# Scan of a Mamba-2 block: the sample's decay factors of all heads made once, in diagonal blocks, and the first set's factors issued one projection later

## The chip, the cores and the metric

The kernel runs on one core of a Trainium2 chip. Five engines with their own instruction queues work side by side: TensorE (PE, with its weight loads shown as PEld), VectorE (DVE), ScalarE (ACT), GpSimd (POOL) and SyncE (SP, which here only issues DMAs). Each takes its instructions in the order in which the program was built. The metric is the device time of one execution in microseconds; the time of a kernel is the median of its runs.

## The reference

One layer of a hybrid trunk for 256 prompt rows and 32 rows of one running stream ("the sample"), 288 rows in all, handled together in fp32.

```python
xn   = rmsnorm(x, norm_mix_pre)
proj = xn @ w_in  # -> [u_pool (1024) | z (2048) | xBC (2560) | dt (32)]
pool = multi-scale trailing-mean mixer on u_pool
ssd  = Mamba-2 mixer: causal conv on xBC, SiLU, exact chunked scan, SiLU gate by z, grouped rmsnorm
x    = x + rmsnorm(concat[pool, ssd] @ w_out, norm_mix_post)
x    = x + rmsnorm(ConvFFN(rmsnorm(x, norm_ffn_pre)), norm_ffn_post)
```

The change is in the scan. For each of 32 heads (64 channels each; two groups of 16 heads share B and C) and for a chunk with running sums `acum` of dt*A:

```python
lmat   = exp(where(causal, acum[l] - acum[s], -inf))
y_diag = einsum(C.B[l, s] * lmat[l, s], x[s] * dt[s])      # within the chunk
y_off  = einsum(C, h_prev, exp(acum))                      # from the state before
```

The sample is a chunk of 32 rows whose state before is an input (`state_ssd`); the prompt starts from zero.

## The kernel before, in words

**Matmuls.** Every fp32 product is made of three: weights and activations are split into a high and a low part, and `mm3` (L145, L146, L147) adds high by high, high by low and low by high. Weights come in DMAs of 1 MB; `split_w` turns each into two pieces of 128x1024, the high part `whi` on ACT (L138) and the low part `wlo` on DVE (L139). There are four buffers for each part. A projection of 256 columns (`project`, K16) takes two DMAs, hence four pieces of 24 matmuls: 96 matmuls on PE.

**Order of the mixer.** First the B/C and first x columns; then seven projections of x (i = 1 to 7), then eight of z (scan steps 8 to 15). After each projection stand, in program order, the evictions of its two accumulators (`ebuf`, L360 and L361 on DVE, for x; `z`, L556, for z), the causal convolution of the tiles of the projection before (`xs_conv`), and `scan(i)`. The convolved x goes to DRAM (`xs_d`) by DMAs on POOL's queue. The framework then orders each engine's instructions by a simulated timeline; weight pieces and evictions have a raised priority.

**The scan.** Heads are taken in eight sets of four. `SCAN_IN` names the steps after which a set's factors are made (`four_in`), `SCAN_OUT` those after which the ready sets, two at a time, are multiplied (`four_out`). `four_in` loads with SP the running sums broadcast to all partitions (`gb`), the state `h0t` and the set's x with rows on partitions (`xw`: two blocks of 128 prompt rows, and a third block of the last 128 rows, of which the last 32 are the sample's). Then, per set:

- ACT: `ce` = Exp of the sample's sums (L487); twelve Relus (L497), per head one of 256, one of 128 and one of 32 columns, `m` = relu(sum of row s - sum of column l); one Exp of the whole `m`, 4 x 416 = 1664 columns (L500). DVE: `ce` times C (L490), `xw` times dt (L493, 768 columns), `m` times the masked B.C products `cbt` (L502, 1664 columns).

`gb`, `xw`, `ce` and `m` have two buffers each, so the third set writes where the first was. `four_out` issues per set sixteen matmuls into `py` (L524), four heads for each of k = 0 to 3: k = 0, 256 prompt columns with `xw` block 0 and `m`; k = 1, 128 columns with block 1; k = 2, the sample's 32 columns with block 2 and `m`; k = 3, the sample's 32 columns with the state and `ce`. They keep their program order on PE, behind the projection. The first run of `four_out` is at step 7: sets 0 and 1, made at steps 5 and 6.

Of the kernel before, what the change touches and what calls it, by code (L numbers as in the profile page):

```python
# [8 lines left out]
F32 = mybir.dt.float32  # L9
F32R = mybir.dt.float32r  # L10
AF = mybir.ActivationFunctionType
ALU = mybir.AluOpType
# [4 lines left out]
P = 128  # L17
TC = {"schedule_with_timeline_sim": True}
D_MODEL = 2048
NP_ = 256  # L20
NS = 32
NT = NP_ + NS
# [3 lines left out]
HEADS = 32  # L26
# [10 lines left out]
MW = 416  # L37
# [6 lines left out]
def body(  # L44
# [25 lines left out]
    act, dve, pool, pe, sp = nc.scalar, nc.vector, nc.gpsimd, nc.tensor, nc.sync  # L70
# [45 lines left out]
        return t[:, 58 : 58 + n * nc_].rearrange("p (k c) -> p k c", k=n)  # L116

    ahead = [0]

    def fetch_w(view, kb, nk, c0, nc_):  # L120
        raw = wpool.tile([P, nk, nc_], F32, tag="raw", name="raw")
# [4 lines left out]
    def split_w(raw, kb, nk, nc_, after=()):  # L126

        out = []
        step = min(nk, 1024 // nc_)
        for k in range(0, nk, step):  # L130
            n = min(step, nk - k)
            hi = wtile("hi", n, nc_)
            lo = wtile("lo", n, nc_)
            with ExitStack() as order:
                order.enter_context(tc.high_priority(offset=ahead[0]))
                for ins in after:
                    order.enter_context(tc.issue_after(ins.ins))
                act.activation(hi, raw[:, k : k + n, :], AF.Copy)  # L138
                dve.tensor_tensor(lo, raw[:, k : k + n, :], hi.bitcast(F32), op=ALU.subtract)  # L139
            out.append([(kb + k + i, hi[:, i, :], lo[:, i, :]) for i in range(n)])  # L140
        return out

# [35 lines left out]
    def blocks_out(d, t, src, pool_, bufs=1, eng=None):  # L178
# [47 lines left out]
    start = ExitStack()  # L226
# [38 lines left out]
    for kb, n in chunks:  # L265
        raw = wpool.tile([P, n, 768], F32, tag="raw", name="raw")
# [19 lines left out]
        for k in range(kb, kb + n):  # L286
# [11 lines left out]
            hi, lo = wtile("hi", 1, 768)[:, 0, :], wtile("lo", 1, 768)[:, 0, :]  # L298
            step = 256 if k < 2 else 768
            for c in range(256 if k == 0 else 0, 768, step):  # L300
                w_hi = act.activation(hi[:, c : c + step], raw[:, k - kb, c : c + step], AF.Copy)
# [9 lines left out]
            for m in range(2 if k == 0 else 0, 6):  # L311
                c = slice(m * P, (m + 1) * P)
# [37 lines left out]
    last_in = [None]  # L350
# [81 lines left out]
    tok = mp.tile([P, 3, 2, HEADS], F32, name="tok")  # L432
    tokd = const.tile([P, 3, HEADS], F32, name="tokd")
    dec_s = mp.tile([HEADS, 4, NS], F32, name="dec_s")
    dve.tensor_copy(dec_s, dec[:, NP_:].unsqueeze(1).broadcast_to([HEADS, 4, NS]))
    dec_s = dec_s.rearrange("h r s -> h (r s)")
    def tok_out():
        p_ = aux([P, 3, 3, HEADS], "ptok")
        jobs = [(2, 2, dec_s)] + [(b, 2, dec[:, P * b : P * b + P]) for b in range(2)]
        for b, (go, o) in enumerate(((0, 0), (256, P), (288, NT - P))):  # L440
# [5 lines left out]
        dve.tensor_copy(tok, p_[:, :, 0:2, :])  # L446
        dve.tensor_copy(tokd, p_[:, :, 2, :])

    tok_out()

# [3 lines left out]
        conv_out(NX + i, bc_in[i], o)  # L454
        bc.append(o)
    b_d = dram.tile([NT, 2 * P], F32, name="b_d")
    cbt = mp.tile([P, 2, MW], F32, name="cbt")
    pool.memset(cbt, 0.0)
    for gi in range(2):
        blocks_out(b_d, gi, bc[gi], mp, 3)  # L460
        p_ = aux([P, MW], "pcb")
        pe.matmul(p_[:, 0:256], bc[gi][:, 0:P], bc[2 + gi][:, 0:NP_], start=True, stop=True)
        pe.matmul(p_[:, 256:384], bc[gi][:, P:NP_], bc[2 + gi][:, P:NP_], start=True, stop=True)
        pe.matmul(p_[:, 384:], bc[gi][:, NT - P :], bc[2 + gi][:, NP_:], start=True, stop=True)
# [3 lines left out]
        dve.tensor_tensor(cbt[P - NS :, gi, 384:], p_[P - NS :, 384:], tri[P - NS :, P - NS :], op=ALU.mult)  # L468


    xs = []
# [2 lines left out]
    def four_in(q):  # L474

        c = slice(2 * P * q, 2 * P * q + 2 * P)
        gb = mp.tile([P, 4, MW], F32, tag="gb", bufs=2, name="gb")
        sp.dma_start(out=gb, in_=g_d[4 * q : 4 * q + 4, :].unsqueeze(0).broadcast_to([P, 4, MW]))
        h0t = mp.tile([P, 2 * P], F32, tag="h0t", bufs=2, name="h0t")
        sp.dma_start(out=h0t, in_=state_ssd[:, c])  # L480
        xw = mp.tile([P, 3, 2 * P], F32, tag="xw", bufs=2, name="xw")
        sp.dma_start(out=xw[:, 0:2, :], in_=xs_d[:NP_, c].rearrange("(b p) c -> p b c", p=P))
        sp.dma_start(out=xw[:, 2, :], in_=xs_d[NT - P :, c])
        ce = mp.tile([P, 4, NS], F32, tag="ce", bufs=2, name="ce")
        m = mp.tile([P, 4, MW], F32, tag="m", bufs=2, name="m")
        with tc.issue_after(last_in[0].ins):
            act.activation(ce, gb[:, :, 384:], AF.Exp)  # L487
            act.activation(elast[:, 4 * q : 4 * q + 4], gb[:, :, MW - 1], AF.Exp)
            cs = bc[2 + q // 4][:, NP_:]
            dve.tensor_tensor(ce, ce, cs.unsqueeze(1).broadcast_to([P, 4, NS]), op=ALU.mult)  # L490
            w = tok[:, :, 1, 4 * q : 4 * q + 4].unsqueeze(3).broadcast_to([P, 3, 4, 64])
            x4 = xw.rearrange("p b (r q) -> p b r q", r=4)
            dve.tensor_tensor(x4, x4, w, op=ALU.mult)  # L493
            for j in range(4):
                h = 4 * q + j
                for b, (lo_, hi_) in enumerate(((0, 256), (256, 384), (384, MW))):
                    act.activation(  # L497
                        m[:, j, lo_:hi_], gb[:, j, lo_:hi_], AF.Relu, bias=tok[:, b, 0, h : h + 1], scale=-1.0
                    )
            act.activation(m, m, AF.Exp, scale=-1.0)  # L500
            gi = q // 4
            got = dve.tensor_tensor(m, m, cbt[:, gi : gi + 1, :].broadcast_to([P, 4, MW]), op=ALU.mult)  # L502
        return xw, h0t, ce, m, got

    def four_out(q, ys, xw, h0t, ce, m, _, after=None):

        ops = []
        for k in range(4):
            for j in range(4):
                c = slice(64 * j, 64 * j + 64)  # L510
                y = ys[j // 2][64 * (j % 2) : 64 * (j % 2) + 64, :]
                if k == 0:
                    ops.append((y[:, 0:256], xw[:, 0, c], m[:, j, 0:256], True, False))
                elif k == 1:
                    ops.append((y[:, 128:256], xw[:, 1, c], m[:, j, 256:384], False, True))
                elif k == 2:
                    ops.append((y[:, 256:], xw[:, 2, c], m[:, j, 384:], True, False))
                else:
                    ops.append((y[:, 256:], h0t[:, c], ce[:, j, :], False, True))
        for y, w_, v_, go, end in ops:  # L520
            with ExitStack() as order:
                if after is not None:
                    order.enter_context(tc.issue_after(after.ins))
                ins = pe.matmul(y, w_, v_, start=go, stop=end)  # L524
# [56 lines left out]
    fours = list(range(NX // 2))  # L581
    gates = list(range(NX))
    done = [-1]
    ready = []
# [757 lines left out]
```

## Time and profile before

| what | value |
|---|---|
| median of 3 runs | 1232.44 us (1232.38 to 1233.84) |
| the profiled execution | 1231.95 us, span 1230.2 us |
| PE busy | 1223.2 us, 99% of the span |
| DVE, ACT, POOL busy | 72%, 55%, 23% |
| projection 7 of x | ends on PE at 130.12 us of the span, where `py` starts; 96 matmuls about 0.122 us apart |
| the four runs of `py` on PE | start at 130.12, 157.85, 196.98, 225.51 us, some 3.7 us each |

The span is the time between the first and the last instruction of the profiled execution; the rest of its time lies around it. A row of a group reads: line, engine, operation, output<-inputs, shape of output<-input, count | busy us, mean ns of one | idle time of the engine just before them and what ended it. A row of a timeline reads: start, duration, engine, line, operation, count of neighbours taken together, and in brackets the idle time before it with its releaser. Engines pipeline their instructions, so the next often starts some 0.1 us before the one ahead has ended; the spacing of starts, not the duration, is what an instruction takes of its engine.

### The profile page before, as it was taken

How to read it: one execution, taken by the hardware profiler on the slowest of the kernel's cores; microseconds unless marked ns; L12 is line 12 of the kernel's file. 1: busy time of each engine (PE TensorE's matmuls, PEld its weight loads, DVE VectorE, ACT ScalarE, POOL GpSimd, SP SyncE). 2: the span in 40 equal slices, each digit the busy share in tenths (PEclk: the TensorE clock that was granted, in tenths of full speed). 3: DMA queues.
4: the chain of work that ended last, by engine and by line, in shares of the span. 5: the costliest groups of instructions: out<-in, count | busy, mean ns of one | idle time of the engine just before them, and what ended most of it. 6: DMA issues, size and time to landing. Idle time of an engine off the chain costs nothing.

```text
span 1230.2 us, 25184 instructions
## 1 busy us (share of the span) xinstructions
PE 1223.2 (99%) x10037; PEld 1212.8 (99%) x10037; DVE 888.5 (72%) x1488; ACT 672.2 (55%) x1013; POOL 277.8 (23%) x428
## 2 busy tenths in 40 slices
PE   9999999999999999999999999999999999999998
PEld 9999999999999999999999999999999999999998
DVE  8999998989654599977776744446777776765555
ACT  8558787546544566654554544334455555454443
POOL 6395442141331200321211200001122121201110
PEclk9999999999999999999999999999999999999999
DMA  9668785466666655776555555555555555576763
GB/s 345 217 202 315 255 281 172 150 244 220 204 234 222 194 174 200 222 211 193 198 183 172 165 186 177 170 193 182 195 172 172 182 184 184 172 248 203 226 189 120
DMA packets 87637, 249.95 MB, mean 203 GB/s; under 512 B 45728, under 2 KB 51936, under 8 KB 65248
## 3 DMA queue, kind: packets, MB, share of 16 engines
q1 hardware_dynamic: 83184, 240.78, 58.5%
q0 software_dynamic: 3760, 7.08, 2.0%
q8 instruction: 78, 1.28, 0.4%
q10 hardware_dynamic: 576, 0.49, 0.1%
q14 instruction: 39, 0.32, 0.1%
HBM read 236.36 MB, written 11.95 MB: 202 GB/s over the span
## 4 chain that ended last, share of the span: by engine, by line
PE 91%; DVE 3%; ACT 3%; issue 1%; DMA 1%; ACTq 0%; DVEq 0%
PE acc L147 29%; PE acc L145 29%; PE acc L146 29%; ACT m L497 2%; DVE wlo L139 1%; PE acc_x L146 1%; PE acc_x L145 1%; PE acc_x L147 1%; ACT whi L138 0%; PE py L524 0%; DMA g_d<-g 0%; DMA gb<-g_d 0%; DVE conv L373 0%; PE low L1183 0%; PE run_a L1185 0%
## 5 line engine op out<-in xcount | busy, mean ns | idle before, releaser
L139 DVE TENSOR_TENSOR wlo<-raw,whi 128x1024 fp32r<-128x1024 f32 (+1 forms) x386 | 460.8, 1196 | 242.3 <-ACT whi L138 241.9
L138 ACT ACTIVATE whi<-raw 128x1024 fp32r<-128x1024 f32 (+1 forms) x386 | 397.2, 1032 | 358.4 <-PE acc L146 290.0
L146 PE MATMUL acc<-hn,whi 128*128 128x288 f32 x1360 | 382.5, 286 | 0.0
L147 PE MATMUL acc<-hn,wlo 128*128 128x288 f32 x1360 | 382.5, 286 | 0.0
L145 PE MATMUL acc<-hn,whi 128*128 128x288 f32 x1360 | 381.8, 286 | 0.1
L146 PEld LDWEIGHTS acc<-hn,whi 128*128 128x128 f32 x1360 | 254.6, 189 | 0.1
L147 PEld LDWEIGHTS acc<-hn,wlo 128*128 128x128 f32 x1360 | 254.6, 189 | 0.0
L145 PEld LDWEIGHTS acc<-hn,whi 128*128 128x128 f32 x1360 | 254.0, 189 | 0.6 <-ACT hn L964 0.5
L145 PE MATMUL acc<-xn,whi 128*128 128x288 f32 x686 | 196.6, 288 | 0.0
L146 PE MATMUL acc<-xn,whi 128*128 128x288 f32 x686 | 195.0, 286 | 0.0
L147 PE MATMUL acc<-xn,wlo 128*128 128x288 f32 x686 | 192.2, 287 | 0.9 <-DVE wlo L139 0.4
L145 PE MATMUL acc<-fa,whi 128*128 128x288 f32 x660 | 188.8, 286 | 0.0
L146 PE MATMUL acc<-fa,whi 128*128 128x288 f32 x660 | 188.8, 286 | 0.0
L147 PE MATMUL acc<-fa,wlo 128*128 128x288 f32 x660 | 188.8, 286 | 0.0
L1014 POOL COPY fc_stage<-ebuf 128x4 f32<-128x4 f32 x88 | 30.2, 343 | 467.4 <-DVE ebuf L1013 467.4
L145 PEld LDWEIGHTS acc<-xn,whi 128*128 128x128 f32 x686 | 129.6, 189 | 1.5 <-issue 0.9
L146 PEld LDWEIGHTS acc<-xn,whi 128*128 128x128 f32 x686 | 129.7, 189 | 0.2
L147 PEld LDWEIGHTS acc<-xn,wlo 128*128 128x128 f32 x686 | 127.9, 189 | 1.7 <-DVE wlo L139 0.9
L145 PEld LDWEIGHTS acc<-fa,whi 128*128 128x128 f32 x660 | 124.7, 189 | 0.0
L146 PEld LDWEIGHTS acc<-fa,whi 128*128 128x128 f32 x660 | 124.7, 189 | 0.0
L147 PEld LDWEIGHTS acc<-fa,wlo 128*128 128x128 f32 x660 | 124.7, 189 | 0.0
L1018 ACT ACTIVATE fc<-ebuf,pf 128x290 f32<-128x290 f32 x88 | 54.6, 623 | 77.3 <-DVE ebuf L1013 77.3
(315 smaller groups left out, 1798.4 us busy)
## 6 DMA issues: line engine op xcount, KB each, us to landing
raw<-in_w_up SPq DMA_DIRECT2D x80, 1024.0 KB, 4.8
raw<-in_w_in SPq DMA_DIRECT2D x38, 1024.0 KB, 5.0
raw<-in_w_down SPq DMA_DIRECT2D x32, 1024.0 KB, 4.8
raw<-in_w_out SPq DMA_DIRECT2D x23, 1024.0 KB, 5.0
raw<-in_w_down SPq DMA_DIRECT2D x16, 768.0 KB, 4.4
raw<-in_w_up SPq DMA_DIRECT2D x8, 896.0 KB, 4.6
gb<-g_d SPq DMA_DIRECT2D x8, 832.0 KB, 6.5
raw<-in_w_first SPq DMA_DIRECT2D x5, 768.0 KB, 7.6
```

The source lines that it names most:

```text
L138: act.activation(hi, raw[:, k : k + n, :], AF.Copy)
L139: dve.tensor_tensor(lo, raw[:, k : k + n, :], hi.bitcast(F32), op=ALU.subtract)
L145: pe.matmul(out, wh, hi, start=start, stop=False)
L146: pe.matmul(out, wh, lo, start=False, stop=False)
L147: pe.matmul(out, wl, hi, start=False, stop=stop)
L497: act.activation(m[:, j, lo_:hi_], gb[:, j, lo_:hi_], AF.Relu, bias=tok[:, b, 0, h : h + 1], scale=-1.0)
L1014: pool.tensor_copy(fc_stage[:, :, :, i], e[:, 256:324].rearrange("p (s c) -> p s c", c=34)[:, :, 0:2])
L1018: act.activation(c, e[:, 0:290], AF.Identity, bias=pf[:, 3, i : i + 1], scale=pf[:, 0, i : i + 1])
```

## The change: what it does

The sample's part leaves `m`, and is made for all heads at once.

- `m` has 4 x 384 columns. Per set, the four Relus of 32 columns go; the Exp and the product with `cbt` have 1536 columns, the product of `xw` with dt 512. The third `xw` block is not loaded; instead `xw_s`, 128x64, holds the set's sample rows, head j on partitions 32j to 32j+31.
- `ms` (128 x 8 sets x 32 columns) holds the sample's factors of all 32 heads, again head j of a set on partitions 32j to 32j+31. Four DMAs on POOL's queue load the sums, and `sample_factors()`, called once at step 6, makes the rest: a subtraction on DVE (L501), Relu and Exp on ACT (L502, L503), two products with `cbs` (B.C of the sample) and one with dt on DVE. Then four ACT copies (L510, 32 partitions x 256 columns) write them into `msz` (128 x 4 x 8 x 32), which was zeroed before: copy j fills rows 32j to 32j+31 of block j alone.
- The k = 2 matmuls read `xw_s` and block j of `msz`. Since the other rows of the block are zero, the same 128 rows of `xw_s` serve all four heads.
- Around it: `tok` loses its third block; `tok_s` (four small ACT copies), `g_s4`, `dt_s4`, `dec_s` and `b_s4` are copies of the sample's columns repeated four times, made on ACT, so that transposes and the B.C product (`pcb`) give the four-fold layout; `tri_s` is the mask, by four POOL copies.

`four_in` is cut into loads (`four_in`) and arithmetic (`four_mul`). At step 5 only set 0's loads are issued. Its arithmetic stands at the start of `scan(6)`, after the second weight piece of projection 6 (`splits[-3]`) and the last eviction. Sets 1 to 7 have both in one step as before.

```diff
@@ split_w
+            splits.append((w_hi, w_lo))
@@ the sample's factors
+    ms = mp.tile([P, 8, NS], F32, name="ms")
+    msz = mp.tile([P, 4, 8, NS], F32, name="msz")
+    pool.memset(msz, 0.0)
+    for j in range(4):
+        pool.dma_start(
+            out=ms[NS * j : NS * (j + 1)],
+            in_=g_d.rearrange("(q j) c -> j q c", j=4)[j, :, 384:].unsqueeze(0).broadcast_to([NS, 8, NS]),
+        )
+
+    def sample_factors():
+        each = lambda t: t.unsqueeze(2).broadcast_to([P, 8, NS])
+        with tc.issue_after(last_in[0].ins):
+            dve.tensor_tensor(ms, each(tok_s[:, 0, :]), ms, op=ALU.subtract)
+            act.activation(ms, ms, AF.Relu)
+            act.activation(ms, ms, AF.Exp, scale=-1.0)
+            for gi in range(2):
+                q4 = slice(4 * gi, 4 * gi + 4)
+                dve.tensor_tensor(ms[:, q4], ms[:, q4], cbs[:, gi : gi + 1, :].broadcast_to([P, 4, NS]), op=ALU.mult)
+            dve.tensor_tensor(ms, ms, each(tok_s[:, 1, :]), op=ALU.mult)
+            for j in range(4):
+                r_ = slice(NS * j, NS * (j + 1))
+                act.activation(msz[r_, j], ms[r_], AF.Copy)
@@ four_in and four_mul
-        xw = mp.tile([P, 3, 2 * P], F32, tag="xw", bufs=2, name="xw")
-        sp.dma_start(out=xw[:, 0:2, :], in_=xs_d[:NP_, c].rearrange("(b p) c -> p b c", p=P))
-        sp.dma_start(out=xw[:, 2, :], in_=xs_d[NT - P :, c])
+        xw = mp.tile([P, 2, 2 * P], F32, tag="xw", bufs=2, name="xw")
+        sp.dma_start(out=xw, in_=xs_d[:NP_, c].rearrange("(b p) c -> p b c", p=P))
+        xw_s = mp.tile([P, 64], F32, tag="xw_s", bufs=2, name="xw_s")
+        sp.dma_start(out=xw_s, in_=xs_d[NP_:, c].rearrange("s (j c) -> j s c", j=4))
...
-        m = mp.tile([P, 4, MW], F32, tag="m", bufs=2, name="m")
-        with tc.issue_after(last_in[0].ins):
+        m = mp.tile([P, 4, MW], F32, tag="m", bufs=2, name="m").rearrange("p j c -> p (j c)")
+        m = m[:, : 4 * CW].rearrange("p (j c) -> p j c", j=4)
+        return gb, xw, xw_s, h0t, ce, m
+
+    def four_mul(q, gb, xw, xw_s, h0t, ce, m, after):
...
-                for b, (lo_, hi_) in enumerate(((0, 256), (256, 384), (384, MW))):
+                for b, (lo_, hi_) in enumerate(((0, 256), (256, CW))):
@@ four_out
-                    ops.append((y[:, 256:], xw[:, 2, c], m[:, j, 384:], True, False))
+                    ops.append((y[:, 256:], xw_s, msz[:, j, q, :], True, False))
@@ scan
+    def four_next(after):
+        q, tiles = loads.pop(0)
+        ready.append((q, four_mul(q, *tiles, after)))
+
     def scan(i):
+        if loads:
+            four_next((*splits[-3], last_in[0]))
...
-            ready.append((q, four_in(q)))
+            loads.append((q, four_in(q)))
+            if i > 5:
+                four_next((last_in[0],))
+        if i == 6:
+            sample_factors()
```

**The first run of `py` on PE.** Behind projection 7 in the order before (`m_1633` is set 0's factors, py_1995 and py_1996 its outputs):

```order
L524 MATMUL py_1995<-m_1633,xw_1629 64x256 x2
L524 MATMUL py_1996<-m_1633,xw_1629 64x256 x2
L524 MATMUL py_1995<-m_1633,xw_1629 64x128 x2
L524 MATMUL py_1996<-m_1633,xw_1629 64x128 x2
L524 MATMUL py_1995<-m_1633,xw_1629 64x32 x2
L524 MATMUL py_1996<-m_1633,xw_1629 64x32 x2
L524 MATMUL py_1995<-ce_1632,h0t_1627 64x32 x2
L524 MATMUL py_1996<-ce_1632,h0t_1627 64x32 x2
```

and now (`m_1659` is set 0's):

```order
L575 MATMUL py_2024<-m_1659,xw_1654 64x256 x2
L575 MATMUL py_2025<-m_1659,xw_1654 64x256 x2
L575 MATMUL py_2024<-m_1659,xw_1654 64x128 x2
L575 MATMUL py_2025<-m_1659,xw_1654 64x128 x2
L575 MATMUL py_2024<-msz_844,xw_s_1656 64x32 x2
L575 MATMUL py_2025<-msz_844,xw_s_1656 64x32 x2
L575 MATMUL py_2024<-ce_1658,h0t_1652 64x32 x2
L575 MATMUL py_2025<-ce_1658,h0t_1652 64x32 x2
```

The count and the places are the same; the third pair of rows reads `msz` where it read `m`.

**ACT around that run.** The last `whi` piece of the first z projection and the third set's factors, in the order now (`m_2073` is the third set's, in the buffer of `m_1659`; `ce_2072` its `ce`):

```order
L139 ACTIVATE whi_2154<-raw_2148 128x1024
L548 ACTIVATE m_2073<-gb_2064,tok_734 128x256
L548 ACTIVATE m_2073<-gb_2064,tok_734 128x128
L548 ACTIVATE m_2073<-gb_2064,tok_734 128x256
L548 ACTIVATE m_2073<-gb_2064,tok_734 128x128
L548 ACTIVATE m_2073<-gb_2064,tok_734 128x256
L548 ACTIVATE m_2073<-gb_2064,tok_734 128x128
L548 ACTIVATE m_2073<-gb_2064,tok_734 128x256
L548 ACTIVATE m_2073<-gb_2064,tok_734 128x128
L551 ACTIVATE m_2073<-m_2073 128x1536
L510 ACTIVATE msz_844<-ms_843 32x256 x4
L538 ACTIVATE ce_2072<-gb_2064 128x128
```

The copies into `msz` are new here; before, the third set's Relus stood behind the same piece too, and no py matmul read what came after them.

**DVE in projection 7.** Between the second eviction of projection 6 and the low part of the fourth weight piece of projection 7, before:

```order
L360 TENSOR_TENSOR ebuf5_674<-acc_1653,rstd_124 128x256
L361 TENSOR_TENSOR ebuf5_674<-acc_1653,rstd_124 128x32
L490 TENSOR_TENSOR ce_1817<-ce_1817,bc_772 128x128
L493 TENSOR_TENSOR xw_1814<-xw_1814,tok_734 128x768
L502 TENSOR_TENSOR m_1818<-m_1818,cbt_795 128x1664
L139 TENSOR_TENSOR wlo_1904<-raw_1897,whi_1903 128x1024
```

and now:

```order
L362 TENSOR_TENSOR ebuf5_674<-acc_1661,rstd_124 128x256
L363 TENSOR_TENSOR ebuf5_674<-acc_1661,rstd_124 128x32
L541 TENSOR_TENSOR ce_1658<-ce_1658,bc_781 128x128
L544 TENSOR_TENSOR xw_1654<-xw_1654,tok_734 128x512
L553 TENSOR_TENSOR m_1659<-m_1659,cbt_808 128x1536
L541 TENSOR_TENSOR ce_1840<-ce_1840,bc_781 128x128
L544 TENSOR_TENSOR xw_1836<-xw_1836,tok_734 128x512
L553 TENSOR_TENSOR m_1841<-m_1841,cbt_808 128x1536
L501 TENSOR_TENSOR ms_843<-tok_s_742,ms_843 128x256
L140 TENSOR_TENSOR wlo_1933<-raw_1926,whi_1932 128x1024
```

Set 0's three products and the subtraction of `ms` have come in ahead of the weight piece.

More of the change, by code (lines that the diff above doesn't have):

```diff
@@ L430, in body, with four_times @@
     dve.tensor_tensor(dec, dec, dt, op=ALU.mult)
-    tok = mp.tile([P, 3, 2, HEADS], F32, name="tok")
+    tok = mp.tile([P, 2, 2, HEADS], F32, name="tok")
     tokd = const.tile([P, 3, HEADS], F32, name="tokd")
-    dec_s = mp.tile([HEADS, 4, NS], F32, name="dec_s")
-    dve.tensor_copy(dec_s, dec[:, NP_:].unsqueeze(1).broadcast_to([HEADS, 4, NS]))
-    dec_s = dec_s.rearrange("h r s -> h (r s)")
+    def four_times(src, name):
+        o = mp.tile([HEADS, 4, NS], F32, name=name)
+        act.activation(o, src.unsqueeze(1).broadcast_to([HEADS, 4, NS]), AF.Copy)
+        return o.rearrange("h r s -> h (r s)")
+    g_s4, dt_s4 = four_times(g[:, 384:], "g_s4"), four_times(dt[:, NP_:], "dt_s4")
+    dec_s = four_times(dec[:, NP_:], "dec_s")
+    tok_s = mp.tile([P, 2, 8], F32, name="tok_s")
     def tok_out():
         p_ = aux([P, 3, 3, HEADS], "ptok")
-        jobs = [(2, 2, dec_s)] + [(b, 2, dec[:, P * b : P * b + P]) for b in range(2)]
-        for b, (go, o) in enumerate(((0, 0), (256, P), (288, NT - P))):
+        jobs = [(2, 2, dec_s)] + [(b, 2, dec[:, P * b : P * b + P]) for b in range(2)] + [(2, 0, g_s4), (2, 1, dt_s4)]
+        for b, (go, o) in enumerate(((0, 0), (256, P))):
             jobs += [(b, 0, g[:, go : go + P]), (b, 1, dt[:, o : o + P])]
@@ L456, in body @@
     b_d = dram.tile([NT, 2 * P], F32, name="b_d")
-    cbt = mp.tile([P, 2, MW], F32, name="cbt")
-    pool.memset(cbt, 0.0)
+    b_s4 = []
+    for gi in range(2):
+        t = mp.tile([P, 4, NS], F32, name=f"b_s4{gi}")
+        act.activation(t, bc[gi][:, NP_:].unsqueeze(1).broadcast_to([P, 4, NS]), AF.Copy)
+        b_s4.append(t.rearrange("p r s -> p (r s)"))
+    CW = 384
+    cbt = mp.tile([P, 2, CW], F32, name="cbt")
+    cbs = mp.tile([P, 2, NS], F32, name="cbs")
+    tri_s = mp.tile([P, NS], F32, name="tri_s")
+    for j in range(4):
+        r_ = slice(NS * j, NS * (j + 1))
+        pool.tensor_copy(tri_s[r_, :], tri[r_, r_])
     for gi in range(2):
@@ L463, in body @@
         pe.matmul(p_[:, 256:384], bc[gi][:, P:NP_], bc[2 + gi][:, P:NP_], start=True, stop=True)
-        pe.matmul(p_[:, 384:], bc[gi][:, NT - P :], bc[2 + gi][:, NP_:], start=True, stop=True)
+        pe.matmul(p_[:, 384:], b_s4[gi], bc[2 + gi][:, NP_:], start=True, stop=True)
         dve.tensor_tensor(cbt[:, gi, 0:128], p_[:, 0:128], tri, op=ALU.mult)
@@ L501, in four_in, with four_out @@
             gi = q // 4
-            got = dve.tensor_tensor(m, m, cbt[:, gi : gi + 1, :].broadcast_to([P, 4, MW]), op=ALU.mult)
-        return xw, h0t, ce, m, got
-    def four_out(q, ys, xw, h0t, ce, m, _, after=None):
+            got = dve.tensor_tensor(m, m, cbt[:, gi : gi + 1, :].broadcast_to([P, 4, CW]), op=ALU.mult)
+        return xw, xw_s, h0t, ce, m, got
+    def four_out(q, ys, xw, xw_s, h0t, ce, m, _, after=None):
         ops = []
```

21 lines of the change are left out of this document (15 added, 6 removed).

## The prediction

> **What bounds the kernel now.** I read first the page's engine totals and its chain of work that ended last.
>
> ```profile
> span 1230.2 us, 25184 instructions
> PE 1223.2 (99%) x10037; PEld 1212.8 (99%) x10037; DVE 888.5 (72%) x1488; ACT 672.2 (55%) x1013; POOL 277.8 (23%) x428
> PE 91%; DVE 3%; ACT 3%; issue 1%; DMA 1%; ACTq 0%; DVEq 0%
> PE acc L147 29%; PE acc L145 29%; PE acc L146 29%; ACT m L497 2%; DVE wlo L139 1%; PE acc_x L146 1%; PE acc_x L145 1%; PE acc_x L147 1%; ACT whi L138 0%; PE py L524 0%; DMA g_d<-g 0%; DMA gb<-g_d 0%; DVE conv L373 0%; PE low L1183 0%; PE run_a L1185 0%
> ```
>
> PE is busy for 99% of the span; no other engine is above 72%. The chain gives ACT's Relus (L497) 2%, some 20 us, which looks like an invitation. So I asked next what PE itself waits for in the stretch that the change touches: the list of waits, PE, 84 to 260 us (its only row), then the windows of 10 us, and the timeline at the two gaps that the windows show.
>
> ```profile
> PE acc L147 <- DVE wlo L139: 0.4, 1, 0.4
> ...
> 100.00:110.00 10.00, 10.00 (x83) 9.95 (x82) 8.26 (x25) 8.26 (x27) 5.66 (x12) 1.00 1.03 372
> ...
> 210.00:220.00 10.00, 9.59 (x76) 9.27 (x75) 8.87 (x9) 9.95 (x12) 0.00 (x0) 1.00 0.32 105
> ...
> 152.26 0.19 PEld L147 LDWEIGHTS acc<-xn,wlo 128*128 128x128 f32 x1 [0.30 <-DVE wlo L139]
> ...
> 213.92 0.39 PE L147 MATMUL acc<-xn,wlo 128*128 128x288 f32 x1 [0.41 <-DVE wlo L139]
> ```
>
> Columns of a window: width; busy us (instructions) of PE, PEld, DVE, ACT, POOL; granted clock; DMA share; GB/s. While the Relus of the first two sets of four heads run (100 to 110), PE is busy for all 10 us. In the whole scan PE loses two short stalls, 0.3 and 0.4 us, both for the low part of a weight piece. **So there is at most about 0.7 us to win here**, and the question is whether the change puts a wait on PE that was not there.
>
> **The change part by part.** *Work removed off the path.* These are the factor instructions, grouped by shape, 80 to 250 us.
>
> ```profile
> L497 ACT ACTIVATE m<-gb,tok 128x256 f32<-128x256 f32 x32 | 15.8, 494 | 0.3 <-PE py L524 0.3
> L497 ACT ACTIVATE m<-gb,tok 128x128 f32<-128x128 f32 x32 | 12.4, 386 | 0.0
> L497 ACT ACTIVATE m<-gb,tok 128x32 f32<-128x32 f32 x32 | 9.8, 306 | 0.0
> L500 ACT ACTIVATE m<-m 128x1664 f32<-128x1664 f32 x8 | 12.6, 1575 | 0.0
> L502 DVE TENSOR_TENSOR m<-m,cbt 128x1664 f32<-128x1664 f32 x8 | 15.1, 1888 | 6.7 <-ACT m L500 6.7
> L493 DVE TENSOR_TENSOR xw<-xw,tok 128x768 f32<-128x768 f32 x8 | 8.2, 1027 | 1.1 <-DMA xw<-xs_d 1.1
> ```
>
> All 32 Relus of 32 columns go: 9.8 us of ACT. The Exp loses 128 of 1664 columns, by the step from 128 to 256 columns (494 less 386 ns) 0.11 us each, 0.9 over eight. The product with cbt loses 128 x 1.13 ns (1888/1664) = 0.14, xw's 256 x 1.34 ns (1027/768) = 0.34: 3.9 us of DVE over eight. Added on ACT are some 13 narrow copies (`four_times`, `b_s4`, `tok_s`, `msz`, estimate 0.3 to 0.5 each by the first and third row: 4 to 6 us) and one Relu and Exp of 256 columns (1.0); on DVE four operations of 256 columns (about 1.6). ACT and DVE end a few us lighter, PE has as many matmuls as before; the four new loads of `ms` stand on POOL's queue (POOL is busy for 23%) long before `sample_factors`; SP's loads keep their places, one of 32 KB in place of one of 128. Since PE waits for none of this in its row, all of it is worth 0 on the path, and at the best the 0.7 us above.
>
> *The wait that is added.* The order of the built program decides. Four heads' py runs on PE as eight matmuls with `m`, four with the sample's factors, four with `ce`. The four in the middle now read `msz`, each its own block, and the ACT copies that write `msz` (L510) stand, at the first run, behind the eight Relus and the Exp of `m_2073`, the third set. That set takes over the buffer of `m_1659` (tag "m", two buffers), which is what those eight py matmuls read. So ACT cannot begin the Relus until PE has done the eight, and PE cannot go on with the ninth until ACT has done Relus, Exp and the first copy. Before, no py matmul waited in this place, since its own `m` held the sample's columns. That the reuse does bind, the tile view of `m` says (who waited for PE's py, and for how long):
>
> ```profile
>   PE py L524: 0.3, 1
> ...
>   ACT m L497: 0.3, 1
> ```
>
> Now its price. PE at the first run before, and ACT's spacing:
>
> ```profile
> 129.90 0.29 PE L147 MATMUL acc<-xn,wlo 128*128 128x288 f32 x1
> 130.12 1.73 PE L524 MATMUL py<-m,xw 128*64 128x256 f32 x24
> 131.67 0.41 PE L524 MATMUL py<-ce,h0t 128*64 128x32 f32 x8
> 131.90 0.63 PE L524 MATMUL py<-m,xw 128*64 128x256 f32 x4
> ...
> L524 PE MATMUL py<-m,xw 128*64 128x128 f32 x48 | 4.0, 273 | 0.0
> ```
> ```profile
> 102.06 3.71 ACT L497 ACTIVATE m<-gb,tok 128x256 f32<-128x256 f32 x12
> 105.67 0.29 ACT L487 ACTIVATE ce<-gb 128x128 f32<-128x128 f32 x1
> ...
> 110.02 1.57 ACT L500 ACTIVATE m<-m 128x1664 f32<-128x1664 f32 x1
> 111.51 0.39 ACT L497 ACTIVATE m<-gb,tok 128x128 f32<-128x128 f32 x1
> ...
> 4.66 0.72 ACT L301 ACTIVATE whi<-raw 128x256 fp32r<-128x256 f32 x2 [0.41 <-DMA raw<-in_w_first]
> ...
> 131.33 1.04 ACT L138 ACTIVATE whi<-raw 128x1024 fp32r<-128x1024 f32 x1
> 132.27 1.90 ACT L497 ACTIVATE m<-gb,tok 128x256 f32<-128x256 f32 x6
> ```
>
> Let T be the start of py (130.12 before). The four `ce` matmuls take 131.90 less 131.67 = 0.23; the twelve ahead 1.55; so PE is free after the eight at T+1.32, and the last of them, 273 ns long at a spacing near 0.1, is done at T+1.5. Twelve Relus take 105.67 less 102.06 = 3.61; without the four of 32 columns (306 ns less the overlap of 0.1 = 0.21 each) eight take 2.77. The Exp's spacing is 111.51 less 110.02 = 1.49, less 0.11 = 1.38. Two copies of 256 columns take 0.72, 0.41 for one and 0.31 more for each that follows. The first block is there at T + 1.5 + 0.1 (semaphore, estimate) + 2.77 + 1.38 + 0.41 = T+6.16: PE stands for 4.8 us. Then three blocks at 0.31 feed three matmuls of 0.06: 0.75 more. **Price 5.6 us.** Lower bound: the copies of a quarter of the partitions are no faster in rows I have, but if a copy's end releases earlier and the semaphore costs nothing, 4.9. Upper bound: the last `whi` piece ahead of the Relus ends 0.6 us after PE's eight matmuls, as 131.33 to 132.27 did (T+2.15 against T+1.5), and each block comes at 0.4: 6.4. Queued behind PE's ninth matmul are the rest of py and the whole first z projection; behind ACT's copies the next `ce` and the weight pieces, for which PE has three pieces in hand. The later three runs read a finished `msz` and pay nothing.
>
> *The first run's factors moved.* Set 0's `ce`, `xw` and `m` products now stand on DVE with set 1's in project 7, ahead of the low part of its fourth weight piece (`wlo_1933`); before only set 1's stood there.
>
> ```profile
> 119.76 0.42 DVE L360 TENSOR_TENSOR ebuf<-acc,rstd 128x256 f32<-128x256 f32 x1
> ...
> 122.19 0.42 DVE L360 TENSOR_TENSOR ebuf<-acc,rstd 128x256 f32<-128x256 f32 x1
> 122.62 0.28 DVE L490 TENSOR_TENSOR ce<-ce,bc 128x128 f32<-128x128 f32 x1
> 122.82 0.95 DVE L493 TENSOR_TENSOR xw<-xw,tok 128x768 f32<-128x768 f32 x1
> 123.69 1.88 DVE L502 TENSOR_TENSOR m<-m,cbt 128x1664 f32<-128x1664 f32 x1
> 125.49 1.22 DVE L139 TENSOR_TENSOR wlo<-raw,whi 128x1024 fp32r<-128x1024 f32 x1
> ```
>
> From the second eviction: 0.43, then twice 0.20 + 0.62 (0.87 less a third, rounded up) + 1.66 (1.80 less 0.14), then `ms` 0.33 (the eviction's width) and the piece 1.22: 6.94 us. The second eviction stood 2.43 behind the first; with one of two conv steps (0.4) now ahead of both, 1.95; the first starts between 118.4 (PE's last matmul of project 6, 96 x 0.122 before 130.12) and 119.76. So the piece is ready between 127.3 and 128.7. PE wants it at 130.12 less 24 x 0.122 plus two matmuls, 127.4. **Stall 0 to 1.3, I take 0.5.** Before, the piece was ready at 125.49 + 1.22 = 126.7, 0.7 us ahead, and DVE is busy for all of 120 to 130 (window below): there is no cover for more.
>
> ```profile
> 120.00:130.00 10.00, 10.00 (x84) 9.97 (x82) 10.00 (x17) 4.71 (x7) 6.06 (x6) 1.00 0.60 201
> ```
>
> *The later stalls.* 152.26 and 213.92 keep their cause; DVE is lighter there (0.5 us per set), but z0's pieces follow a stalled ACT. Net 0.1, between -0.7 and +0.5.
>
> **Sum:** 5.6 + 0.5 + 0.1 = +6.2 on the profiled execution of 1231.95 (span 1230.2): 1238.15. The median, 1232.44, is 0.49 above that execution: **1238.6 us**. Bounds: 4.9 + 0 - 0.7 = +4.2 and 6.4 + 1.3 + 0.5 = +8.2, so 1236.6 to 1240.6.
>
> **The rivals.** *The array also slows down after the stall.* 4.8 us without a matmul is longer than any gap of this profile, and how the array restarts shows only at the start:
>
> ```profile
> 0.85 2.90 PE L261 MATMUL idle<-const-float32-1.0 128*128 128x128 f32 x12 [0.85 <-PEq L1316]
> 4.12 2.00 PE L292 MATMUL acc<-xs,raw 128*128 128x288 f32 x4 [0.37 <-DVE xs L290]
> 5.74 0.50 PE L145 MATMUL acc<-xn,whi 128*128 128x288 f32 x1
> ...
> 0.00:10.00 10.00, 8.78 (x48) 7.92 (x49) 4.54 (x11) 6.18 (x14) 3.09 (x32) 1.00 0.78 268
> ```
>
> Until 5.74 a matmul of 288 columns takes 0.50 instead of 0.29, at half pace, though the granted clock reads 1.00 for this window too. From 0.85 on that is 4.9 us at half pace, 2.4 us lost. If the same follows the stall: 1238.6 + 2.4 = 1241.0. For it: the stall is long. Against: a gap of 0.4 us before 4.12 says nothing on when the pace drops. Chance 0.25. [...] The first rows agree with a slow start; no run shown here has a gap that tests the fall.
>
> *The copies are not late* (the change does not wait as I read it): if the third set's Relus did not have to wait for py, they would still follow a `whi` piece of 1.04 that PE's last matmuls (129.90) set free, so the first block would come at 131.1 + 2.77 + 1.38 + 0.41 = T+5.5; the wait vanishes only if the copies overtake the Relus, from T-3 on. Against: ACT takes its instructions in the built order. A part-stall of 0 to 3 us gives 1232.4 to 1235.4. Chance 0.08.
>
> *Faster.* The chain's 20 us of Relus are a real path: its 96 lose 9.8 of 38 us busy, a quarter of 20 = 5 us, so 1227.4. It decides if PE is found waiting where ACT ran the Relus; the window 100 to 110 with PE at 10.00 speaks against. Chance 0.04.
>
> **How the numbers follow.** Forecast 0.60, half pace 0.25, copies not late 0.08, faster 0.04, and 0.03 for more than all that (both stalls at their bounds and half pace, above 1242.6). 0.2%, 2.5 us, is about what a measurement can tell from no change. Slower takes the forecast, half pace, the excess, and a little of the part-stalls: 0.89; same 0.07; faster 0.04. The range reaches from 1235.2, under the lower bound by a missed hiding of about a microsecond, to 1242.6, half pace on the upper part of the second stall.
>
> **What would show it.** Right: one gap of about 5 us on PE within the first py, released by ACT `msz` L510, with the Relus of the third set (L548) on ACT in it, and three short waits behind; below it a wait of some tenths for `wlo` near 127; the other three py phases as before. Records of 0.50 after the gap would make it the half-pace case. Wrong: PE in that py without a gap over 1 us, or a gap before its first matmul (factors not ready) instead of after its eighth.

## The result

The changed kernel takes **1239.96 us** (median of 4 runs, 1238.57 to 1241.03) against 1232.41 for the kernel before (1230.74 to 1233.84): ratio 1.0066, 95% interval 1.0054 to 1.0079. It is slower by 7.55 us. Its profiled execution took 1241.03 us, with a span of 1239.3. Two executions among the experiments below, one of the second and one of the third, took some 1830 us at a clock of 0.654 and are left out of every number here.

The page of the changed kernel (span; busy time of each engine; chain by engine):

```profile
span 1239.3 us, 25192 instructions
PE 1227.2 (99%) x10037; PEld 1217.0 (98%) x10037; DVE 886.4 (72%) x1491; ACT 668.9 (54%) x996; POOL 287.4 (23%) x436
PE 94%; DVE 2%; DMA 1%; ACT 1%; issue 1%; POOL 0%; DVEq 0%; ACTq 0%
```

ACT and DVE did become lighter, by 3.3 and 2.1 us, and the span grew by 9.1. PE's list of waits names the places:

```profile
PE py L575 <- issue: 4.8, 1, 4.8
...
PE acc L149 <- DVE wlo L140: 0.7, 1, 0.7
```

PE's timeline at the first run of `py` (start, duration, instruction, idle time before it). The releaser of the long wait is not named here ("issue"); ACT's rows below give it.

```profile
129.52 0.39 PE L149 MATMUL acc<-xn,wlo 128*128 128x288 f32 x1 [0.74 <-DVE wlo L140]
...
132.17 1.52 PE L575 MATMUL py<-m,xw 128*64 128x256 f32 x16
138.53 1.59 PE L575 MATMUL py<-msz,xw_s 128*64 128x32 f32 x7 [4.84 <-issue]
...
143.49 0.39 PE L147 MATMUL acc<-xn,whi 128*128 128x288 f32 x1
```

ACT's timeline over the same stretch:

```profile
132.15 1.06 ACT L139 ACTIVATE whi<-raw 128x1024 fp32r<-128x1024 f32 x1 [0.94 <-PE acc L148]
133.74 2.88 ACT L548 ACTIVATE m<-gb,tok 128x256 f32<-128x256 f32 x8 [0.53 <-PE py L575]
136.64 1.48 ACT L551 ACTIVATE m<-m 128x1536 f32<-128x1536 f32 x1
138.03 1.72 ACT L510 ACTIVATE msz<-ms 32x256 f32<-32x256 f32 x4
```

The first eight matmuls (each leaves two records, hence 16) start at 132.17; the ninth starts at 138.53, when the first copy into `msz` has ended (138.03 + 0.41). In between ACT waits for PE (0.53), makes the third set's eight Relus and its Exp, and copies. From the start of `py` to the first matmul of the z projection it is 11.32 us, against 3.65 before (130.12 to 133.77).

A part of that is not waiting. The windows of 1 us show the granted clock in the third column from the right:

```profile
136.00:137.00 1.00, 0.00 (x0) 0.00 (x0) 1.00 (x5) 0.97 (x3) 1.00 (x3) 0.51 0.88 349
...
141.00:142.00 1.00, 1.00 (x8) 1.00 (x6) 1.00 (x3) 0.31 (x1) 0.84 (x3) 0.50 1.06 440
142.00:143.00 1.00, 1.00 (x16) 1.00 (x13) 1.00 (x4) 0.57 (x2) 0.32 (x2) 0.58 1.12 336
143.00:144.00 1.00, 1.00 (x23) 0.96 (x18) 1.00 (x6) 0.84 (x3) 0.00 (x0) 1.00 0.90 342
```

The clock is 0.50 from 136.0 to about 142.8, for 6.8 us, of which PE works from 138.5 on. All four runs list a mean clock of 0.997; the 26 runs of the kernel before that stand beside the first four experiments list 0.999 or 1.0.

**Where the 9.1 us of span went**, by the starts of the same work in the two traces:

| stretch | before | after | difference |
|---|---|---|---|
| start to `prs` (first projections) | 37.1 | 38.1 | +1.0 |
| `prs` to the first `py` | 93.0 | 94.0 | +1.0 |
| first `py` to the z projection | 3.65 | 11.32 | +7.67 |
| to the second `py` | 24.1 | 23.7 | -0.35 |
| second to third `py` | 39.1 | 39.1 | 0 |
| third to fourth `py` | 28.5 | 27.85 | -0.7 |
| fourth `py` to the end | 1004.7 | 1005.1 | +0.4 |

`prs` and `psum_g` are short matmuls at the head and in the later part of the mixer, taken as marks. I do not count the first row as the change's: the first matmuls run at half pace (one every 0.24 us here until 9.5 us, then every 0.12), and the end of that stretch lies at 5.7 us in the profile of before, at 9.7 here and between 4 and 7 in the profiles of the first four experiments (8 to 11 matmuls in each us from 5 or 6 us on, 5 or fewer in the us before), so it moves from one profile to another. `prs` starts at 37.1 in the profile of before, at 38.1 here, and at 35.9 to 37.7 in the experiments' profiles; the two do not go together in all of them (36.0 in the third experiment, whose matmuls reach full pace between 5 and 6 us, against 37.1 before with 5.7), so a part of this row is open. The last row, +0.4, stays unexplained. The executions of the kernel before spread by 3.5 us for these reasons or others, which bounds what the comparisons below can tell.

### The profile page after: what moved, and what is told of

The parts are those of the page before. It is cut to its first block, busy times and chain, and to the rows that moved or that the text cites. A ratio compares the mean times of both kernels' runs of the same rounds, so it can differ in the third digit from the quotient of the medians.

```text
span 1239.3 us, 25192 instructions
## 1 busy us (share of the span) xinstructions
PE 1227.2 (99%) x10037; PEld 1217.0 (98%) x10037; DVE 886.4 (72%) x1491; ACT 668.9 (54%) x996; POOL 287.4 (23%) x436
## 4 chain that ended last, share of the span: by engine, by line
PE 94%; DVE 2%; DMA 1%; ACT 1%; issue 1%; POOL 0%; DVEq 0%; ACTq 0%
PE acc L147 30%; PE acc L149 30%; PE acc L148 30%; PE py L575 1%; PE acc_x L149 1%; PE acc_x L147 1%; PE acc_x L148 1%; DMA sx<-xs_d 1%; ACT m L548 0%; DVE wlo L140 0%; PE py_a L575 0%; PE low L1244 0%; PE run_a L1246 0%; POOL xs_d L186 0%; ACT whi L139 0%
```

## The experiments

Theory A: PE waits inside the first `py` because the copies into `msz` are late; behind ACT's Relus and Exp stands a second cause, DVE's product of `ms` with dt (L507), which ended 1.1 us before the copies began. DVE's row in the changed kernel:

```profile
136.55 0.41 DVE L507 TENSOR_TENSOR ms<-ms,tok_s 128x256 f32<-128x256 f32 x1
```

The rivals were: the place of the copies on ACT alone (B), the deferral of the first set (E), the new layout itself (D). The first four experiments stand beside one set of 26 runs of the kernel before (median 1231.03), the last four beside another (1231.48).

### The third set behind the copies

```diff
+    made = [None]
...
-                act.activation(msz[r_, j], ms[r_], AF.Copy)
+                made[0] = act.activation(msz[r_, j], ms[r_], AF.Copy)
...
-                four_next((last_in[0],))
+                four_next((last_in[0], made[0]) if i == 7 else (last_in[0],))
```

> The changed kernel, with the third set's ACT work (ce, Relus, Exp) ordered behind the four copies into msz; nothing is left out and DVE's order is the same. Theory A (the Relus and the Exp are the last wait, but DVE's product of ms with dt, which ended at 136.96, 1.1 us before the copies began at 138.03, is right behind it): the first block comes at 136.96 + 0.45 = 137.4 instead of 138.5, PE's gap in the first py shrinks from 5.0 to about 3.9 us, the granted clock may still fall to 0.50, and the time is 1238.3 to 1239.5 us. Rival B (the place behind the Relus and the Exp is the whole cause, as the prediction priced it): no gap over 1 us, no fall of the clock, 1233.3 us.

Measured: 1239.17 us, ratio 1.0058 (1.0044 to 1.0073); clock 0.997 in all four runs. Timelines of ACT and DVE, and PE's wait:

```profile
PE py L577 <- issue: 3.8, 1, 3.8
```
```profile
134.90 1.73 ACT L512 ACTIVATE msz<-ms 32x256 f32<-32x256 f32 x4 [3.77 <-DVE ms L509]
```
```profile
134.46 0.41 DVE L509 TENSOR_TENSOR ms<-ms,tok_s 128x256 f32<-128x256 f32 x1
```

ACT now idles 3.77 us for DVE's product with dt, and PE's wait went from 4.8 to 3.8 us. A holds, B falls: taking the Relus and the Exp out of the way takes 1 us off the wait, because the product with dt is nearly as late. The first `py` gets only 0.5 us shorter (10.8 us to the z projection, against 11.3), since all of what follows the wait now runs at a clock of 0.50. The time hardly moves: the kernel gives that back ahead of the second `py`, where PE now waits for a `wlo`; the third set's factors run later there.

```profile
163.00 0.39 PE L149 MATMUL acc<-xn,wlo 128*128 128x288 f32 x1 [1.03 <-DVE wlo L140]
```

### The sample's factors one step earlier

```diff
-        if i == 6:
+        if i == 5:
             sample_factors()
```

> The changed kernel, with sample_factors() called one step earlier (step 5), so that DVE's four operations and ACT's copies stand before or in projection 7. Nothing is left out. Theory A: msz is finished some 4 us before py needs it, so there is no gap in py and no fall of the clock; the wait for wlo near 128 shrinks from 0.9 to about 0.5 us, since one subtraction of 0.33 us has gone from ahead of it; 1232.0 to 1233.0 us, the same as before. Rival C (the lighter Relus win something once the stall is gone): 1231.0 us or less. Rival D (the new layout itself costs, whatever the time of the factors): over 1234.5 us.

Measured: 1232.06 us (10 runs), ratio 1.0005 (0.9996 to 1.0014): no difference from the kernel before can be told, and the loss is gone. PE's rows (the first is the only wait of the scan):

```profile
128.55 0.39 PE L149 MATMUL acc<-xn,wlo 128*128 128x288 f32 x1 [1.46 <-DVE wlo L140]
...
131.20 1.52 PE L575 MATMUL py<-m,xw 128*64 128x256 f32 x16
...
132.99 0.63 PE L575 MATMUL py<-m,xw 128*64 128x256 f32 x4
```

`py` runs through: the second set's matmuls start 1.79 us after the first set's, as before (130.12 to 131.90). ACT's copies are done 9.5 us before `py`, where I had expected 4:

```profile
119.92 1.73 ACT L510 ACTIVATE msz<-ms 32x256 f32<-32x256 f32 x4 [0.84 <-DVE ms L507]
```

A holds in the main; D falls. The other number that I missed is the wait for `wlo`: it is 1.46 us, not 0.5. Between the two evictions of projection 6 DVE now has the product with dt and one conv step more (2.76 us from one to the other, 1.99 in the changed kernel), and all that follows on DVE is later by that. C is not decided: the two short waits of before (152.26 and 213.9) are gone, 1.0 us by the starts of the second and fourth `py`, and the new wait has taken their place.

### The first set not deferred

```diff
-            if i > 5:
-                four_next((last_in[0],))
+            four_next((last_in[0],))
```

> The changed kernel, with the first set's factors back at step 5, as before the change; sample_factors stays at step 6. Nothing is left out. Theory A: two effects. The wait for wlo near 128 goes (0.9 us), and DVE's product with dt comes about 2.5 us earlier, while the built order has put the copies ahead of the Relus here: first block near T+3.5 instead of T+6.4, gap in py 2.2 us instead of 5.0. 1234.5 us if the clock holds, 1236.4 if it falls. Rival E (the deferral alone makes the stall): no gap over 0.5 us, 1232.5 us.

Measured: 1233.84 us (9 runs, 1233.01 to 1235.67), ratio 1.0022 (1.0013 to 1.0031). PE's rows, DVE's at the first of them, and ACT's at the second:

```profile
113.40 0.39 PE L149 MATMUL acc<-xn,wlo 128*128 128x288 f32 x1 [1.33 <-DVE wlo L140]
...
132.48 1.51 PE L575 MATMUL py<-msz,xw_s 128*64 128x32 f32 x7 [0.21 <-issue]
```
```profile
110.01 1.76 DVE L553 TENSOR_TENSOR m<-m,cbt 128x1536 f32<-128x1536 f32 x1 [1.55 <-ACT m L551]
```
```profile
131.96 1.73 ACT L510 ACTIVATE msz<-ms 32x256 f32<-32x256 f32 x4 [0.18 <-DVE ms L507]
```

The median is 0.7 us under A's, and the parts are others. The first block of `msz` comes 0.2 us late instead of 2.2, and the three others arrive 0.44 us apart, so `py` takes 5.2 us in place of 3.65. And there is a wait that I had not seen: in projection 6 DVE waits 1.55 us for ACT's Exp of the first set with a `wlo` piece behind it, and PE stands for 1.33. Without the deferral `py` is still late by 1.6 us, so E's time (1232.5) does not come out. But E has its gap right: PE stands 0.21 us in `py` instead of 4.84. The deferral puts 2.48 us of the first set's products ahead of `ms` on DVE in projection 7 (122.97 to 125.45 in the changed kernel); DVE's product with dt starts 0.8 us behind the start of `py` here and 4.4 us behind it there, and the copies stand ahead of the third set's Relus here and behind them there. The next experiment shows that the deferral alone makes no gap in `py` either. So the long wait needs both: the factors at step 6 and the deferral. The parts make 1.3 + 1.6 - 1.0 for the old stalls = 1.9 us, about as in the profiled execution (1233.08); other runs reach 1235.67, and that is not explained.

### The deferral alone

The kernel before with `four_in` cut in two, as in the change; `m` keeps its 1664 columns.

```diff
     def scan(i):
+        if loads:
+            four_next((*splits[-3], last_in[0]))
...
-            ready.append((q, four_in(q)))
+            loads.append((q, four_in(q)))
+            if i > 5:
+                four_next((last_in[0],))
```

> The kernel before, with only the first set's arithmetic deferred behind the second piece of the next projection; the sample's factors stay in m. Nothing is left out. Theory A: py has no gap, the wait for wlo in projection 7 is 0.9 to 1.6 us (the products are as wide as before, so DVE has 0.85 us more ahead of the piece than in the changed kernel, without the subtraction's 0.33), 1233.3 to 1234.0 us. Rival F (hidden, DVE catches up): 1232.4 us. Rival E again: over 1237 us.

Measured: 1235.24 us (9 runs, 1232.39 to 1237.04), ratio 1.0028 (1.0018 to 1.0037). In the profile, an execution of 1232.39 us whose clock is 1.0:

```profile
128.67 0.39 PE L149 MATMUL acc<-xn,wlo 128*128 128x288 f32 x1 [2.00 <-DVE wlo L140]
```

`py` has no gap, as A says, so E falls as it stands, and F falls with the wait; the wait in projection 7 is 2.0 us, 0.4 over the upper end I gave, and the median is 1.2 us over my upper end of 1234.0. The spread is the surprise: five of the nine runs list a clock of 0.998 and take 1235.24 to 1237.04 us, the other four 0.999 or 1.0 and 1232.39 to 1234.30.

### How long a gap the clock bears

The kernel before, with DVE work ahead of the fourth `wlo` piece of projection 7, in two sizes. This is the first; the second has 1664 in place of 1250, the whole of `m`:

```diff
-                for ins in after:
+                if dialed:
+                    pieces[0] += 1
+                for ins in (*after, *(dialed if pieces[0] == 4 else ())):
...
+    def dial(got):
+        m, x = (t.rearrange("p j c -> p (j c)") for t in (got[-2], got[0]))
+        m = m[:, :1250]
+        with tc.high_priority(offset=3000):
+            with tc.issue_after(got[-1].ins):
+                dialed.append(dve.tensor_tensor(x, x, x, op=ALU.max))
+            dialed.append(dve.tensor_tensor(m, m, m, op=ALU.max))
...
+        if i == 7:
+            dial(ready[1][1])
```

> The kernel before, with two idle DVE operations (x = max(x, x) on the second set's xw and m, 768 and 1250 columns) ahead of the fourth wlo piece of projection 7, so that PE stands for about 2.5 us there; nothing else is added or left out. It asks how long a gap lets the granted clock fall. Theory I (the clock falls about 2.6 us after the last matmul, as it did at 136.0 and 134.0 in the changed kernel and in e1): the fall comes in some executions only, mean clock 0.998 to 1.0, 1233.5 us without and 1236 with it. [...]

> The same with 768 and 1664 columns: PE stands for about 3.0 us. Theory I: the clock falls in every execution, mean 0.998 or less, 1236.5 us. [...]

Measured: 1235.18 us (6 runs), ratio 1.0029 (1.0017 to 1.0041), and 1235.66 us (5 runs), 1.0027 (1.0015 to 1.0039). The gaps came out at 2.16 and 2.37 us. In the profile of the first the clock fell, after PE had resumed; in that of the second, with the longer gap, it did not:

```profile
129.44 0.39 PE L150 MATMUL acc<-xn,wlo 128*128 128x288 f32 x1 [2.16 <-DVE wlo L142]
...
129.00:130.00 1.00, 0.56 (x4) 0.56 (x5) 1.00 (x2) 0.00 (x0) 0.00 (x0) 1.00 0.00 0
130.00:131.00 1.00, 1.00 (x7) 1.00 (x6) 1.00 (x3) 0.00 (x0) 0.00 (x0) 0.55 0.77 139
131.00:132.00 1.00, 1.00 (x6) 1.00 (x6) 1.00 (x2) 0.00 (x0) 0.80 (x2) 0.50 0.81 295
132.00:133.00 1.00, 1.00 (x6) 1.00 (x5) 1.00 (x5) 0.00 (x0) 1.00 (x2) 0.50 1.03 418
133.00:134.00 1.00, 1.00 (x7) 0.81 (x7) 1.00 (x2) 0.26 (x1) 0.61 (x2) 0.75 1.08 381
```
```profile
128.93 0.39 PE L150 MATMUL acc<-xn,wlo 128*128 128x288 f32 x1 [2.37 <-DVE wlo L142]
...
129.00:130.00 1.00, 1.00 (x8) 1.00 (x9) 1.00 (x2) 0.00 (x0) 0.00 (x0) 1.00 0.43 66
130.00:132.00 2.00, 2.00 (x18) 1.77 (x18) 2.00 (x6) 0.43 (x1) 1.30 (x3) 1.00 0.85 283
```

By the listed clocks 0.998 was reached in two of six and three of five runs; in the second kernel these took 1235.66 to 1235.97 us and the two others 1233.63 and 1233.77, so one fall costs about 2 us. (Of the ten profiled executions, the seven whose windows between 124 and 140 us show no low stretch list 0.999 or 1.0, that of the first kernel here 0.998, those of the changed kernel and of the first experiment 0.997; so I read a listed 0.998 as a fall.) Theory I as I wrote it (a fixed 2.6 us after the last matmul) falls: the fall came 2.8 us after PE stopped in one and not at all in the other.

PE's longest wait in projection 7 and the first `py` by its row, beside the stretch at a clock of 0.50 by the windows, in these profiles:

| profile | longest wait of PE, us | clock 0.50 |
|---|---|---|
| the changed kernel | 4.84 | 136.01 to 142.84, 6.8 us |
| the first experiment | 3.81 | 134.08 to 140.91, 6.8 us |
| the second kernel here | 2.37 | none |
| the first kernel here | 2.16 | 130.09 to 133.51, 3.4 us |
| the deferral alone | 2.00 | none |
| the factors one step earlier | 1.46 | none |

So the length of the gap alone does not decide: the clock fell with 2.16 us and stayed with 2.37. What else decides is not shown by these runs, and only the profiled executions can be laid out like this. Once PE worked again, the clock came back after 4.1 to 5.5 us (129.44 to 133.51 here, 138.53 to 142.84 in the changed kernel, 135.42 to 140.91 in the first experiment).

### The first half of the change alone, and in time

The edits of the second and the third experiment together:

```diff
-            if i > 5:
-                four_next((last_in[0],))
-        if i == 6:
+            four_next((last_in[0],))
+        if i == 5:
             sample_factors()
```

> The sample's factors made once, at step 5, without the deferral of the first set: the first half of the change alone, with its factors in time. Nothing is left out. Theory A: no gap in py; the wait for wlo in projection 7 goes; but, as in the run with the factors at step 6 and no deferral, DVE's product of the first set waits for ACT's Exp near 112 us with a wlo piece of projection 6 behind it, 1.3 to 1.9 us on PE. The two old short stalls behind the first py (0.3 and 0.4 us with what follows them, 1.0 together in the earlier runs) are gone: 1231.0 to 1232.0 us where the kernel before has 1231.0. Rival F (that wait was an accident of the other order): 1230.0 us.

Measured: 1233.53 us, ratio 1.0012 (1.0003 to 1.0021), some 1.5 us above the expectation. Its only wait in the scan is the one expected, 1.43 us in projection 6:

```profile
114.18 0.39 PE L149 MATMUL acc<-xn,wlo 128*128 128x288 f32 x1 [1.43 <-DVE wlo L140]
```

F falls. The profiled execution took 1232.25; why the median lies 1.3 above it is open. Two of the eleven runs list 0.998, which I read as a fall; the profiled execution, with a gap of 1.43 us, lists 0.999, and how long PE stood in those two is not on record. Most of the upper runs list 0.999 or 1.0.

### The second set's product behind the weight piece

On top of the earlier factors, DVE's product of the second set with `cbt` is issued in `scan(7)` behind the low part of the fourth piece:

```diff
-            got = dve.tensor_tensor(m, m, cbt[:, gi : gi + 1, :].broadcast_to([P, 4, CW]), op=ALU.mult)
+            got = None if q == 1 else last_mul(q, m)
...
+        if i == 7:
+            q, got = ready.pop()
+            with tc.issue_after(splits[-1][1].ins):
+                ready.append((q, (*got[:-1], last_mul(q, got[-2]))))
```

> The changed kernel with sample_factors() at step 5 (as in e2), and DVE's product of the second set with cbt moved from ahead of the fourth wlo piece of projection 7 to behind it. Nothing is left out. Theory A: that piece comes 1.7 us earlier, the wait of 1.5 us in e2 goes, the product is done by T-1 and py does not wait: 1232.1 - 1.5 = 1230.6 us, 0.4 us under the kernel before. Rival G (the piece waits for its buffer or its load, not for DVE): still 1.5 us of wait, 1232.1 us. Rival H (the product is late for py): a wait ahead of py's first matmul, 1231.5 us or more.

Measured: 1231.35 us (11 runs), ratio 0.9998 (0.9990 to 1.0007). DVE's piece and product, and the start of `py`, which now has no wait ahead of it or in it:

```profile
126.79 1.22 DVE L140 TENSOR_TENSOR wlo<-raw,whi 128x1024 fp32r<-128x1024 f32 x1
127.93 1.76 DVE L537 TENSOR_TENSOR m<-m,cbt 128x1536 f32<-128x1536 f32 x1
```
```profile
130.72 1.52 PE L580 MATMUL py<-m,xw 128*64 128x256 f32 x16
```

G and H fall: PE's list has no wait from 20 us to 1218 us, where the closing part of the kernel begins to wait for DVE. By the traces the stage is 1.0 us shorter than before (from `prs` to the second `psum_g`, 252.6 - 37.7 = 214.9 against 253.0 - 37.1 = 215.9), and the expected 0.4 us below the kernel before is not to be told from no change by these runs. It is the best order of the change that I found, and it only ties.

## Why the prediction came out as it did

The time was in the range and on the right side, 1239.96 against 1238.6; but the likeliest case was not the one that happened. The rival with half pace was (1241.0 worked out).

- **Nothing to win.** Right. With every wait of the stage gone, the stage is 1.0 us shorter; I had allowed 0.7. ACT and DVE got lighter and the time of the kernel did not follow.
- **The added wait.** Right in place, in mechanism and in its parts: Relus from T+1.57 (1.6 worked out), Exp to copy 1.39 (1.38), ninth matmul at T+6.36 (6.16), PE standing for 5.0 us by the starts (4.8), 4.84 by its row. The size that was off is the three blocks that follow. I took 0.31 us from two copies of 256 columns at the start of the kernel; the four copies into `msz` take 1.72 together, 0.44 apart. Together with the pace (below) the term came out at 7.7 us, over its upper bound of 6.4. No run shows the 0.1 us for the semaphore by itself; in the changed kernel the Relus start 0.05 us after the eighth matmul's record ends (133.69 to 133.74) and the ninth matmul 0.09 us after the first copy's (138.44 to 138.53).
- **What the prediction did not name** is the second cause behind the first. The prediction spoke as if the copies had only to overtake the Relus. DVE's product with dt ended only 1.1 us before the copies began, and the first experiment, which does let them overtake, gains 1 us of PE's 5.
- **The deferred set.** The mechanism was right, the sizes at or past my ends: PE waits 0.74 us by its row (0.5 taken), where the bound was 1.3, and without `ms` but with other work ahead 1.46, with the wide products 2.0. What I had wrong is its part in the long wait. I priced the deferral as a second wait by itself; but without it, and with the factors still at step 6, PE stands 0.21 us in `py` and not 4.84, and the time is 1233.84, not 1239.96. It is one of the two causes. What it saves is small: with the new layout and no deferral, PE waits 1.3 to 1.4 us in projection 6 instead of in projection 7.
- **The later stalls.** I netted them to +0.1; they went, -1.0 (the lower bound was -0.7). The lighter DVE is enough for that, since in the last experiment both are gone though PE stands nowhere ahead of them. It is not shown to be the reason in the changed kernel: the first stall is gone in the kernels with the old `m` too, where PE stood in projection 7 (23.7 us from the z projection to the second `py` in the deferral alone and in both kernels with added DVE work, the same as in the changed kernel, against 24.1 before).
- **The pace.** I gave 0.60 to an array that keeps its pace and 0.25 to half pace. The clock fell in every one of the four runs (each lists 0.997). My reason against it, that no gap of this profile tests the fall, was a reason for an even chance, not for a low one. In the profile the fall, at 136.01, came 2.3 us after the eighth matmul's record had ended and 2.5 us before the ninth started. The price was near: a loss of 2.4 was worked out; of the rest of `py`, 4.96 us against 2.30 before, 1.1 us are the blocks' pace and about 1.5 the clock.

The sum with what was measured: 7.7 in `py` + 0.9 for `wlo` and its restart - 1.0 = 7.6, against a difference of medians of 7.55. The agreement is closer than the traces allow: the two profiled executions differ by 8.1 us without the table's first row, with its unexplained +0.4. That the likeliest case came within 1.4 us is luck in part: the first `py` was 2.1 us dearer than its term and `wlo` 0.4, the later stalls 1.1 cheaper.

## What to carry to other kernels

Work that is shared by many steps and made once has one first user: look at what is queued ahead of it on each engine at that moment, and at the second latest input as well as the latest, since removing one wait only uncovers the next. When an engine's buffer is taken over by later work, that work waits for the consumer, and whatever is queued behind it and is also needed by that consumer closes a loop of waits. Work that is moved later to make room is also work in the queue ahead of whatever comes next: the deferral here made no gap in `py` alone, and the long one together with the late factors. In a kernel bound by PE, a gap can cost more than itself: here one of 2.16 us was followed by 3.4 us at a clock of 0.50, one of 2.37 us in another kernel was not. Price it with the pace at which the array resumes.

## What the hardware showed that I had not expected

- The granted clock fell to 0.50 with gaps of 4.84, 3.81 and 2.16 us on PE and not with one of 2.37 us. The fall came 2.3, 2.5 and 2.8 us after PE had stopped, in the last case (130.09, PE back at 129.44) only after it had resumed. The clock stayed low for 6.8, 6.8 and 3.4 us.
- At the start of the kernel the matmuls also run at half pace (0.24 us apart in place of 0.12), yet the windows there show a granted clock of 1.00: the trace's list of clock stretches begins only with the end of the half pace, at 5.7 us in the profile of before and 9.7 in that of the changed kernel. Between the profiles `prs`, behind this stretch, moves by 2.2 us.
- Four ACT copies of 32 partitions x 256 columns take 0.41 us each and start 0.44 apart, as long as an operation on all 128 partitions (0.42 for the Relu of 128x256 on `ms`): a quarter of the partitions cost the same here.
